# Row scales spread over the partitions by four small products with the identity, and row tiles loaded two to a buffer

## The chip, the cores and the metric

The kernel runs on one core of one Trainium2 chip. The metric is the device time of one execution in microseconds (us). Before the change three runs gave 842.63, 842.73 and 844.46 us; the median is 842.73 us.

## The reference, cut to what matters

One layer of an encoder trunk over 2048 rows (frames) of 1024 channels, all in float32:

```
h    = x * rsqrt(mean(x*x, axis=-1) + 1e-6) * norm_w        # RMSNorm, one scale per row
proj = h @ w_in                                             # 1024 -> 3348 columns, four branches
y_a, y_b, y_c, y_d = conv(...), gla(...), pool(...), ssd(...)
x    = x + concat(y_a, y_b, y_c, y_d) @ w_out
out  = x * rsqrt(mean(x*x, axis=-1) + 1e-6) * final_norm_w
```

The change touches only the first line: the scale `rsqrt(mean(x*x) + 1e-6)` of each row, and how it gets to where the projection's results are scaled. The branches (short causal convolutions, two chunked recurrences over chunks of 64 rows, moving means) matter only as the work that follows.

## The kernel before, in words

The 2048 rows are worked in two segments of 1024, each in two halves of 512 rows (f = 0 and 1). A float32 product is made as three products of "high" and "low" parts (`mm3`, L183): ACT casts an operand to its high part (L140) and DVE subtracts to get the low part (L141). A projection block (`block_ch`, L272) is 24 such products of 512 columns that put 128 channels by 512 rows into one of three accumulators (`acc`, L77). A block's result stays in its accumulator until DVE or ACT has moved it out (`evac`, L210).

The first segment doesn't wait for the row scales. Its operands are x * norm_w (`prep_first`, L521), and the scale is multiplied on behind the product: by row when rows lie on the partitions (`rt`, [row, tile], L621 and L624), and along the free axis, the same on all partitions, when channels lie on the partitions (`rb`, used in `evac` at L213 and L215). To get both, `scale_first` (L201) squares and sums four tiles of 128 rows on ACT (L199), takes 1/sqrt in a dozen small DVE steps (`rsqrt`, L121) and writes `rt` (L206). For `rb` it then sends the 512 numbers to a scratch tensor `rd` in DRAM by a DMA of POOL's queue (L207), and reads them back, the same 2 KB to each partition, by a DMA of SP's queue (L208), which waits until the first has landed.

The row tiles come in by `load_x` (L537). There are two buffers (tags "bt" and "cc", 8 KB a partition each), one tile of 4 KB a partition in each at a time, so that the third tile's load waits until the first tile's squares are done, and so on. The order in which the program emits the start is: x and weights of half 0 in pieces (L549 to L559), the q block's weights (L560), the first piece of half 1 (L561), two row tiles (L562), the parameters `prm` with the identity (L563), the products of the values and gates of half 0 (`kv_outer`, L566), two more row tiles (L581), `scale_first(0)`, the rest of half 1 (L584), and `scale_first(1)` with its four row tiles (L585). Then the segment loop runs: q block of half 0 and its `evac` with `rb` (L630), `kv_outer` of half 1, q block of half 1 and its `evac`, the B blocks, and so on.

For the second segment, whose operands are normalised before the product, `row_scale` (L228) sums the squares in the middle of the first segment and sends the scales to `rd` (L237), and `row_scale_bc` (L239) reads them back along the free axis (L241) when `prep` (L244) is about to use them (L595 and L746).

Each engine and each DMA queue works in order, and the order is fixed when the program is built: a planner takes the emitted instructions by their place in the program and by its own estimate of when each is ready, and so may put a later one ahead of an earlier one that isn't ready. `later` (L257) delays the emission of a piece by some projection blocks.

Of the kernel before, what the change touches and what calls it, by code (L numbers as in the profile page):

```python
# [35 lines left out]
           p_u=1808, p_z=2064, s_z=2320, xs=2576, B=2832, C=3088, dt=3344)  # L36
# channel-major blocks of 128 projection columns, in the order in which they are used
BLOCKS = ([('q', 0), ('B', 0), ('B', 1), ('k', 0), ('xs', 0), ('xs', 1), ('C', 0), ('C', 1)]
# [3 lines left out]

# columns of the packed per-channel parameters
PC = {}
# [9 lines left out]
def tile_hybrid_trunk(ctx: ExitStack, tc: tile.TileContext, xtok, xT, wkv, wch, wpu, wz, wo, pw_, nw, par, gw, fnw, out):  # L54
# [18 lines left out]
    def nm(s):  # L73
        uid[0] += 1
        return f"{s}_{uid[0]}"
# [9 lines left out]

# [1 line left out]
    # the tensor engine is kept at work until its first operands are there  # L87
    wz_ = px.tile([P, 512], F32, tag="xtok", name="warm")
# [27 lines left out]
    yd = dr.tile([SEQ // P, P, KD, P], F32, name="yd")  # L116
    rd = dr.tile([4, HALF], F32, name="rd")
    wd = dr.tile([2, P, D], F32, name="wd")

# [1 line left out]
    def rsqrt(ssq, inv, n, v=None):  # L121
        """1/sqrt(ssq*inv + EPS) of a [128, n] tile (or 1/sqrt(v)), times RS"""
        y = psm.tile([P, 16], F32, tag="ny", name=nm("ny"))[:, :n]
        a = psm.tile([P, 16], F32, tag="na", name=nm("na"), bufs=1)[:, :n]
        if v is None:
            v = psm.tile([P, 16], F32, tag="nv", name=nm("nv"), bufs=1)[:, :n]
            vec.tensor_scalar(v, ssq, inv, EPS, ALU.mult, ALU.add)  # L127
        vec.tensor_single_scalar(a.bitcast(I32), v.bitcast(I32), 1, ALU.logical_shift_right)
        vec.tensor_scalar(y.bitcast(I32), a.bitcast(I32), -1, 0x5f3759df, ALU.mult, ALU.add)
        for c in (3.0, 12.0, 768.0):  # L130
            if n == 1:
                vec.scalar_tensor_tensor(a, y, v, y, ALU.mult, ALU.mult)
            else:
                vec.tensor_tensor(a, y, v, ALU.mult)
                vec.tensor_tensor(a, a, y, ALU.mult)
            vec.scalar_tensor_tensor(y, a, c, y, ALU.subtract, ALU.mult)
        return y
# [5 lines left out]
    def load_w(src, n):  # L143
        """one packed weight tile [128, n] in its two parts"""
        raw = pw.tile([P, 1024], F32, tag="raw", name=nm("raw"), bufs=3)[:, :n]
        sp.dma_start(raw, src)
        return split_w(raw, n)
# [7 lines left out]
    def fold_pu(j):  # L155
        """p_u's projection block j with the pool's channel mixing folded into it, to wd"""
        raw = px.tile([P, KD, P], F32, tag="xT", name=nm("raw"))
# [25 lines left out]
    def mm3(o, ops):  # L183
        """o = sum of lhsT^T rhs over (lh, ll, rh, rl), each product in its three parts"""
        last = len(ops) - 1
# [15 lines left out]
    def scale_first(f, xs):  # L201
        """the 1/rms of four tiles of rows: [row, tile] to rt, and along the free axis on every partition to rb"""
        ssq = psm.tile([P, 4], F32, tag="ssq", name=nm("ssq"))
        square_sums(xs, ssq)
        rstd = rsqrt(ssq, 1.0 / D, 4)
        vec.tensor_single_scalar(rt[:, f, :], rstd, 1.0 / RS, ALU.mult)  # L206
        nc.gpsimd.dma_start(rd[f].rearrange("(j p) -> p j", p=P), rt[:, f, :])  # L207
        sp.dma_start(rb[:, f, :], rd[f:f + 1, :].to_broadcast([P, HALF]))  # L208

    def evac(s, f, dst, o, scale=None):  # L210
        """dst = o * scale of a channel-major block; the first segment's blocks still miss their rows' 1/rms"""
        if s == 0 and scale is None:
# [8 lines left out]
    def evac_silu(s, f, dst, o):  # L221
# [3 lines left out]
        else:  # L225
            act.activation(dst, o, AF.Silu)

    def row_scale(hf):  # L228
        """the rows' 1/rms of half hf (of four) to rd"""
        ssq = psm.tile([P, 4], F32, tag="ssq", name=nm("ssq"))  # L230
# [4 lines left out]
        rstd = rsqrt(ssq, 1.0 / D, 4)  # L235
        vec.tensor_single_scalar(rstd, rstd, 1.0 / RS, ALU.mult)
        nc.gpsimd.dma_start(rd[hf].rearrange("(j p) -> p j", p=P), rstd)  # L237

    def row_scale_bc(hf):  # L239
        rb = gen()[:, :512]  # L240
        sp.dma_start(rb, rd[hf:hf + 1, :].to_broadcast([P, HALF]))  # L241
        return rb

    def prep(s, f, rb):  # L244
        """normalised activations of half f of segment s, channel-major, in two parts"""
        hh, hl = hT[f] = big(f)
# [10 lines left out]
    def later(n, fn):  # L257
        """fn is emitted behind the n-th projection block from here"""
        queue.append([n, fn])
# [12 lines left out]
    def block_ch(f, w):  # L272
        """a projection block, channel-major: [128 channels, 512 tokens] of half f"""
        o = acc()
# [6 lines left out]
    def block_tok(tt, ws, n):  # L281
        """a projection block, token-major: [128 tokens, n columns]"""
        o = acc()[:, :n]
# [8 lines left out]
    def gate(f, kv):  # L292
        """decays [channel, token] of the keys of half f to the ends of their chunks, and the chunks' own decays"""
        lp = tr()
# [38 lines left out]
    def dt_chain(kv, wt, aD):  # L333
        """SSD step weights wt [tok, tt, head] and chunk decays aD [any, parity, tt, head]"""
        def t32(n):
# [31 lines left out]
    def ssd_conv(s, f, i, ps_):  # L367
        """silu(conv) of xbc block i for one half, channel-major"""
        xin = gen()
# [9 lines left out]
    def chunk_loop(kv, kt, q, aG, aD, bt, wxs, dxs, cc):  # L379
        """the updates of a token tile's two chunks, and a step later their outputs"""  # L380
        rows = (slice(0, CH), slice(CH, P))
# [51 lines left out]
    def spill(s, f, blk, y):  # L433
        """channel-major y [128, 512] of half f to block blk of the mixed channels"""
        t0 = s * TT + f * 4
# [34 lines left out]
    def pool_u(s, j, f, o):  # L470
        """mean over each window less the position's own value, of u already mixed"""
        lo_, hi_ = slice(0, 64), slice(64, 128)
# [42 lines left out]

# [1 line left out]
    # the first segment's products take x * norm_w and are scaled by the rows' 1/rms behind, which need not be waited for  # L517
    rb = pseg.tile([P, 2, HALF], F32, tag="rb", name="rb")
    rt = psm.tile([P, 2, 4], F32, tag="rt", name="rt", bufs=1)

    def prep_first(f, i, tag, n=2):  # L521
        """the first segment's activations of half f, channel tiles 2i and 2i+1, n at a time"""
        xt = px.tile([P, 2, HALF], F32, tag="xT", name=nm("xT"))
# [13 lines left out]
    def load_x(j, tag):  # L537
        xk = pseg.tile([P, D], F32, tag=tag, name=nm("xk"))
        sp.dma_start(xk, xtok[j])
        return xk  # L540

# [7 lines left out]
    for k0, k1 in order:  # L549
        next(x1[k0 // 2])  # L550
        k = k0
        while k < k1:
# [6 lines left out]
            k += n  # L559
    wq = load_w(wch[BLOCKS.index(('q', 0))], D)  # L560
    next(prep_first(1, 0, "wxs"))  # L561
    xh = [load_x(j, ("bt", "cc")[j % 2]) for j in range(2)]  # L562
    sp.dma_start(prm, par)  # L563
    act.activation(ea, pcol('alog', 0, 4), AF.Exp)

    def kv_outer(hs, o):  # L566
        """the values and gates of four token tiles, one k at a time"""
        for k in range(KD):
# [11 lines left out]
    kv_outer(hT[0], kvp)  # L580
    xh += [load_x(2 + j, ("bt", "cc")[j % 2]) for j in range(2)]  # L581
    scale_first(0, xh)
    for i in range(1, 4):
        next(prep_first(1, i, ("wxs", "dxs")[i % 2]))  # L584
    scale_first(1, [load_x(4 + j, ("bt", "cc")[j % 2]) for j in range(4)])  # L585

# [6 lines left out]
    for s in range(NSEG):  # L593
# [7 lines left out]
        wt = psm.tile([P, TT, 4], F32, tag="wt", name=nm("wt"), bufs=1)  # L601
        es, rsts = [], []
        cur = {} if s else {('q', 0): wq}
# [10 lines left out]
        for f in range(2):  # L614
# [14 lines left out]
            later(2, lambda f=f: rsts.append(gate(f, kv)))  # L629
            evac(s, f, q[:, f * HALF:(f + 1) * HALF], get('q', 0, f), 32.0 ** -0.5)  # L630
        later(2, lambda: gate_decay(rsts, aG, es))
# [75 lines left out]

        # gated outputs of the two recurrent branches
        wzt = []
# [30 lines left out]

        # pool, the first half of all its blocks before the second
        wp = []
        ab = {}
        for f in range(2):
# [4 lines left out]
            for j in range(2):  # L749
# [4 lines left out]
                if f == 1 and s + 1 < NSEG:  # L754
                    wk[0] = load_kv((0, 1)) if j == 0 else wk[0] + load_kv((2,))
# [1 line left out]
    fw = pseg.tile([P, D], F32, tag="kv", name="fw")  # L757
# [18 lines left out]
    def project(tt, c0, c1, i):  # L776
        """output columns c0:c1 of token tile tt with the residual, and their square sum; running mean square + EPS"""
        yh, yl, xk, r, ot, sq = tiles[tt]
# [35 lines left out]
def _pack(x, norm_w, w_in, conv_a_w, gla_gate_w, gla_gate_b, gla_norm_w, pool_w, pool_scale, ssd_conv_w, ssd_conv_b,  # L814
          ssd_dt_bias, ssd_a_log, ssd_d, ssd_norm_w, w_out, final_norm_w):
    """the inputs laid out for the kernel"""
    f = np.float32
# [72 lines left out]
```

## Time and profile before

| | |
|---|---|
| median of 3 runs | 842.73 us (842.63 to 844.46) |
| span of the profiled execution | 844.6 us |
| PE (matmul) busy | 816.5 us, 97% of the span |
| DVE busy | 499.3 us, 59% |
| ACT busy | 275.4 us, 33% |
| POOL busy | 6.3 us, 1% |
| mean granted clock of TensorE | 0.988 of full speed |
| DMA | 86.71 MB, mean 103 GB/s |

The profile is of one execution, whose own time is its span of 844.6 us; it is 1.9 us above the median of the runs. PE is the engine that sets the time. The slices of the profile cut the span in 40 pieces of 21.1 us; a digit is a busy share in tenths. A row of a timeline reads: start, duration, engine, source line, operation, output <- inputs, shape, count, and in brackets the idle time before it and what ended that. PE instructions overlap, so that the distance between starts, not the duration, says what one costs. A float32 product that isn't cut in parts shows as two records.

### The profile page before, as it was taken

To read this page: it belongs to the slowest core of one execution; us is meant where nothing else is said; L and a number is where in the kernel's file an instruction comes from. 1 tells how busy PE (TensorE), PEld (TensorE's weight loads), DVE (VectorE), ACT (ScalarE), POOL (GpSimd) and SP (SyncE) were. 2 spreads that over 40 slices of the span, in tenths; PEclk is the share of its full clock that TensorE was granted. 3 is DMA by queue.
4 is the path that set the end of the run, shared out by engine and by line. 5 is a ranking of instruction groups with operands and counts; after the bars stand their busy time and mean duration, and the time that the engine had idled before them with its cause. 6 is when DMAs were issued, how large, how long until landed. Compare 5 with 4: busy or idle time off the path is not lost.

```text
span 844.6 us, 11158 instructions
## 1 busy us (share of the span) xinstructions
PE 816.5 (97%) x4272; PEld 675.4 (80%) x4272; DVE 499.3 (59%) x1253; ACT 275.4 (33%) x487; POOL 6.3 (1%) x22
## 2 busy tenths in 40 slices
PE   7975999999999999999999999999999999999996
PEld 6954888787878888998888787878888888888885
DVE  5545757674754588955846464544578765555544
ACT  5633444242212332355545211213334332122211
POOL 0000000000000000000000000000000000000000
PEclk9987999999999999999999999999999999999999
DMA  8664101144741033523011102111045654443221
GB/s 283 231 158 115 47 29 51 51 148 119 117 135 38 26 116 113 190 61 125 26 51 50 50 27 75 45 44 38 25 162 165 181 191 151 150 150 124 101 100 50
DMA packets 38836, 86.71 MB, mean 103 GB/s; under 512 B 3872, under 2 KB 17536, under 8 KB 38784
## 3 DMA queue, kind: packets, MB, share of 16 engines
q1 hardware_dynamic: 38656, 86.00, 32.4%
q8 instruction: 33, 0.54, 0.3%
q14 instruction: 19, 0.16, 0.1%
q0 software_dynamic: 128, 0.01, 0.0%
HBM read 68.16 MB, written 17.83 MB: 102 GB/s over the span
## 4 chain that ended last, share of the span: by engine, by line
PE 86%; DMA 8%; DVE 2%; ACT 2%; issue 1%; SPq 1%; DVEq 0%; ACTq 0%
PE acc L187 27%; PE acc L189 27%; PE acc L188 27%; DMA xtok<-in_xtok 3%; DMA rd<-rt 2%; PE up L391 1%; PE tr L638 1%; PE oy L399 1%; PE oy L403 1%; DMA rb<-rd 1%; DMA xT<-in_xT 1%; DMA xk<-in_xtok 1%; ACT xtok L199 1%; DMA raw<-in_wkv 1%; PE tr L167 0%
## 5 line engine op out<-in xcount | busy, mean ns | idle before, releaser
L187 PE MATMUL acc<-bl,wh 128*128 128x512 f32 x640 | 255.6, 399 | 6.1 <-DVE nv L127 6.1
L189 PE MATMUL acc<-bh,wl 128*128 128x512 f32 x640 | 251.3, 393 | 0.0
L188 PE MATMUL acc<-bh,wh 128*128 128x512 f32 x640 | 251.1, 392 | 0.0
L187 PEld LDWEIGHTS acc<-bl,wh 128*128 128x128 f32 x640 | 121.3, 190 | 31.9 <-issue 6.3
L189 PEld LDWEIGHTS acc<-bh,wl 128*128 128x128 f32 x640 | 121.1, 189 | 26.0
L188 PEld LDWEIGHTS acc<-bh,wh 128*128 128x128 f32 x640 | 121.4, 190 | 23.9
L188 PE MATMUL acc<-bh,yh 128*128 128x512 f32 (+1 forms) x264 | 101.0, 383 | 0.0
L189 PE MATMUL acc<-bh,yl 128*128 128x512 f32 (+1 forms) x264 | 101.0, 383 | 0.0
L187 PE MATMUL acc<-bl,yh 128*128 128x512 f32 (+1 forms) x264 | 101.0, 383 | 0.0
L140 ACT CAST wh<-raw 128x1024 fp32r<-128x1024 f32 (+3 forms) x57 | 55.9, 982 | 119.6 <-PE acc L188 106.1
L141 DVE TENSOR_TENSOR wl<-raw,wh 128x1024 fp32r<-128x1024 f32 (+3 forms) x57 | 64.5, 1135 | 36.9 <-ACT wh L140 33.6
L187 PE MATMUL acc<-wl,bh 128*128 128x512 f32 (+1 forms) x192 | 69.0, 359 | 0.0
L189 PE MATMUL acc<-wh,bl 128*128 128x512 f32 (+1 forms) x192 | 68.5, 357 | 0.0
L188 PE MATMUL acc<-wh,bh 128*128 128x512 f32 (+1 forms) x192 | 68.4, 356 | 0.0
L376 DVE SCALAR_TENSOR_TENSOR g<-g,prm,g 128x512 f32<-128x512 f32 x72 | 53.7, 751 | 8.2 <-ACT g L374 6.7
L189 PEld LDWEIGHTS acc<-bh,yl 128*128 128x128 f32 x264 | 49.6, 188 | 9.7
L188 PEld LDWEIGHTS acc<-bh,yh 128*128 128x128 f32 x264 | 49.6, 188 | 9.7
L187 PEld LDWEIGHTS acc<-bl,yh 128*128 128x128 f32 x264 | 49.6, 188 | 9.7
L785 DVE TENSOR_TENSOR r<-acc,xk 128x512 f32<-128x512 f32 (+1 forms) x33 | 22.3, 675 | 56.2 <-PE acc L189 55.0
L786 ACT ACTIVATE xk<-r 128x512 f32<-128x512 f32 (+1 forms) x33 | 20.4, 618 | 86.8 <-issue 66.6
L187 PEld LDWEIGHTS acc<-wl,bh 128*128 128x128 f32 x192 | 36.1, 188 | 5.3 <-issue 0.3
L189 PEld LDWEIGHTS acc<-wh,bl 128*128 128x128 f32 x192 | 36.1, 188 | 5.2
(191 smaller groups left out, 872.8 us busy)
## 6 DMA issues: line engine op xcount, KB each, us to landing
raw<-in_wch SPq DMA_DIRECT2D x36, 512.0 KB, 3.4
xk<-in_xtok SPq DMA_DIRECT2D x24, 512.0 KB, 3.6
yr<-yd SPq DMA_DIRECT2D x16, 512.0 KB, 4.2
out<-ot SPq DMA_DIRECT2D x30, 256.0 KB, 2.2
xT<-in_xT SPq DMA_DIRECT2D x14, 512.0 KB, 4.4
xtok<-in_xtok SPq DMA_DIRECT2D x8, 512.0 KB, 6.4
raw<-in_wz SPq DMA_DIRECT2D x8, 512.0 KB, 3.9
yd<-g SPq DMA_DIRECT2D x16, 256.0 KB, 2.8
```

Source lines behind the costliest of these rows:

```text
L140: act.copy(hi, raw)
L141: vec.tensor_sub(lo, raw, hi.bitcast(F32))
L187: pe.matmul(o, lhsT=lh, rhs=rl, start=i == 0, stop=False)
L188: pe.matmul(o, lhsT=lh, rhs=rh, start=False, stop=False)
L189: pe.matmul(o, lhsT=ll, rhs=rh, start=False, stop=i == last)
L199: act.activation(xk, xk, AF.Square, accum_out=ssq[:, j:j + 1])
L376: vec.scalar_tensor_tensor(t, xin[:, k:k + 512], pcol('scw', 4 * i + k), t, ALU.mult, ALU.add)
L391: pe.matmul(o[:, CH + g * P:CH + (g + 1) * P], lhsT=bt[r, tt, g, :], rhs=wxs[r, tt, g * P:(g + 1) * P], start=True, stop=True)
L399: pe.matmul(oy[rows[i], 0:256], lhsT=q[:, tok[i]], rhs=st[i][0], start=True, stop=True)
L403: pe.matmul(oy[rows[i], 256 + g * P:256 + (g + 1) * P], lhsT=cc[:, g, tok[i]], rhs=st[i][1][:, gs], start=True, stop=True)
L785: vec.tensor_tensor(r[:, cs], o, xk[:, cs], ALU.add)
L786: act.activation(xk[:, cs], r[:, cs], AF.Square, accum_out=sq[:, i:i + 1])
```

## The change

The scales no longer go through DRAM. A new function makes four products: the left operand is one column of the scales [128 rows, 1], repeated 128 times along the free axis, and the right one is the identity; the result holds the 128 scales along the free axis on every partition. ACT copies the 512 results to SBUF. It is called four times: in the segment loop behind each q block of the first segment, and in `row_scale_bc` for each half of the second. A buffer of `load_x` now holds two row tiles, so that four row tiles fit at a time; their bytes and number of DMAs stay. The first four row tiles are loaded ahead of `kv_outer(hT[0], kvp)`, and `prm` ahead of the first piece of half 1.

```diff
...
-    rd = dr.tile([4, HALF], F32, name="rd")
...
         vec.tensor_single_scalar(rt[:, f, :], rstd, 1.0 / RS, ALU.mult)
-        nc.gpsimd.dma_start(rd[f].rearrange("(j p) -> p j", p=P), rt[:, f, :])
-        sp.dma_start(rb[:, f, :], rd[f:f + 1, :].to_broadcast([P, HALF]))
+
+    def along_rows(dst, cols):
+        tp = tr()
+        for j in range(4):
+            pe.matmul(tp[:, j * P:(j + 1) * P], lhsT=cols[:, j:j + 1].to_broadcast([P, P]), rhs=ident,
+                      start=True, stop=True)
+        act.copy(dst, tp)
...
+    scales = {}
+
     def row_scale(hf):
...
-        vec.tensor_single_scalar(rstd, rstd, 1.0 / RS, ALU.mult)
-        nc.gpsimd.dma_start(rd[hf].rearrange("(j p) -> p j", p=P), rstd)
+        scales[hf] = psm.tile([P, 4], F32, tag="rs", name=nm("rs"))
+        vec.tensor_single_scalar(scales[hf], rstd, 1.0 / RS, ALU.mult)
...
     def row_scale_bc(hf):
         rb = gen()[:, :512]
-        sp.dma_start(rb, rd[hf:hf + 1, :].to_broadcast([P, HALF]))
+        along_rows(rb, scales[hf])
         return rb
...
     def load_x(j, tag):
-        xk = pseg.tile([P, D], F32, tag=tag, name=nm("xk"))
-        sp.dma_start(xk, xtok[j])
-        return xk
+        xk = pseg.tile([P, 2, D], F32, tag=tag, name=nm("xk"))
+        for i in range(2):
+            sp.dma_start(xk[:, i, :], xtok[j + i])
+        return [xk[:, 0, :], xk[:, 1, :]]
...
     wq = load_w(wch[BLOCKS.index(('q', 0))], D)
+    sp.dma_start(prm, par)
     next(prep_first(1, 0, "wxs"))
-    xh = [load_x(j, ("bt", "cc")[j % 2]) for j in range(2)]
-    sp.dma_start(prm, par)
+    xh = load_x(0, "bt") + load_x(2, "cc")
...
     kv_outer(hT[0], kvp)
-    xh += [load_x(2 + j, ("bt", "cc")[j % 2]) for j in range(2)]
     scale_first(0, xh)
...
-    scale_first(1, [load_x(4 + j, ("bt", "cc")[j % 2]) for j in range(4)])
+    scale_first(1, load_x(4, "bt") + load_x(6, "cc"))
...
-            evac(s, f, q[:, f * HALF:(f + 1) * HALF], get('q', 0, f), 32.0 ** -0.5)
+            qs.append(get('q', 0, f))
+            if s == 0:
+                along_rows(rb[:, f, :], rt[:, f, :])
+            evac(s, f, q[:, f * HALF:(f + 1) * HALF], qs[f], 32.0 ** -0.5)
...
```

## Rows read from the trace of the kernel before

**Rows 1.** The page's slices of 21.1 us: PE's busy share, in tenths.
```profile
PE   7975999999999999999999999999999999999996
```

**Rows 2.** Timeline of PE, 27 to 85 us: blocks and waits.
```profile
27.63 0.29 PE L572 MATMUL acc<-wh,bh 128*128 128x276 f32 x1
...
39.76 0.40 PE L187 MATMUL acc<-bl,wh 128*128 128x512 f32 x1
...
45.26 0.60 PE L296 MATMUL tr<-prm,kv 128*16 128x128 f32 x4
51.91 0.76 PE L187 MATMUL acc<-bl,wh 128*128 128x512 f32 x1 [6.05 <-DVE nv L127]
...
56.31 0.42 PE L188 MATMUL acc<-bh,wh 128*128 128x512 f32 x1
...
74.84 0.79 PE L309 MATMUL tr<-rst,gst 96*128 96x512 f32 x1 [9.00 <-ACT rst L301]
...
80.12 0.46 PE L189 MATMUL acc<-bh,wl 128*128 128x512 f32 x1
```

**Rows 3.** Timeline of DVE, 25 to 72 us.
```profile
25.75 1.23 DVE L141 TENSOR_TENSOR bl<-xw,bh 128x1024 fp32r<-128x1024 f32 x1 [0.19 <-ACT bh L140]
...
35.12 0.17 DVE L206 TENSOR_SCALAR rt<-ny 128x4 f32<-128x4 f32 x1
...
51.07 0.69 DVE L215 SCALAR_TENSOR_TENSOR q<-acc,rb 128x512 f32<-128x512 f32 x1 [12.44 <-DMA rb<-rd]
...
71.30 0.69 DVE L215 SCALAR_TENSOR_TENSOR q<-acc,rb 128x512 f32<-128x512 f32 x1 [9.26 <-DMA rb<-rd]
```

**Rows 4.** The chain that ended last, 35 to 72 us: start, us, what.
```profile
35.59 10.72 DMA rd<-rt
...
55.59 9.84 DMA rd<-rt
65.45 5.83 DMA rb<-rd
```

**Rows 5.** Timeline of SP's queue, 12 to 47 us.
```profile
13.70 0.43 SPq L563 DMA_DIRECT2D prm<-in_par  x1
...
22.51 1.37 SPq L539 DMA_DIRECT2D xk<-in_xtok  x2
...
46.33 0.33 SPq L208 DMA_DIRECT2D rb<-rd  x1
```

**Rows 6.** Landing times of L539's DMAs, the row tiles, in us.
```profile
DMA to landing us min/median/max: 3.4/5.5/10.3
```

**Rows 7.** Stretches: engines busy (x count), PEclk, DMA share, GB/s.
```profile
16.00:20.00 4.00, 3.54 (x28) 3.54 (x29) 3.85 (x6) 2.03 (x3) 0.00 (x0) 1.00 1.00 390
...
40.00:44.00 4.00, 4.00 (x19) 3.29 (x18) 0.00 (x0) 0.00 (x0) 0.00 (x0) 1.00 0.00 0
...
52.00:56.00 4.00, 4.00 (x10) 3.13 (x11) 3.66 (x14) 2.78 (x4) 0.41 (x1) 0.50 0.73 298
```

**Rows 8.** Timeline of ACT, 21 to 48 us: squares of row tiles.
```profile
29.69 1.07 ACT L199 ACTIVATE xk<-xk 128x1024 f32<-128x1024 f32 x1
...
46.56 1.06 ACT L199 ACTIVATE xk<-xk 128x1024 f32<-128x1024 f32 x1 [7.83 <-DMA xk<-in_xtok]
```

**Rows 9.** Timeline of PE: four float32 products of 128 columns, and its neighbour.
```profile
208.12 1.16 PE L167 MATMUL tr<-g,raw 128*128 128x128 f32 x8
209.04 0.48 PE L187 MATMUL acc<-bl,wh 128*128 128x512 f32 x1
```

**Rows 10.** Chain in order of time: four transposes of 128 columns.
```profile
94.93 0.44 PE tr L638 x4
```

**Rows 11.** Line L363: loads of a left operand repeated along its free axis.
```profile
L363 PEld LDWEIGHTS tr<-d,prm x8: 185/189/192, 83.7 to 402.6; 128*128 128x128 f32 x8
```

**Rows 12.** Timeline of DVE, segment 1: the last operands of half 1.
```profile
367.59 1.36 DVE L141 TENSOR_TENSOR bl<-hf,bh 128x512 fp32r<-128x512 f32 x2
```

**Rows 13.** Timeline of PE, segment 1: last product of half 1's first block.
```profile
369.00 0.39 PE L189 MATMUL acc<-wh,bl 128*128 128x276 f32 x1
```

More of the change, by code (lines that the diff above doesn't have):

```diff
@@ L601, in tile_hybrid_trunk @@
         wt = psm.tile([P, TT, 4], F32, tag="wt", name=nm("wt"), bufs=1)
-        es, rsts = [], []
+        es, rsts, qs = [], [], []
         cur = {} if s else {('q', 0): wq}
```

## The prediction

> **What bounds the kernel now.** I read the page's slices first: PE is at nine tenths or more in 36 of 40 slices, and at seven, seven and five in the first, third and fourth [rows 1]. The change works in just that place, so everything else was read there. The timeline of PE then shows the two holes. After the q block of half 1, which ends at 45.26 us, come four short transposes, and then PE stands for 6.05 us before the first B block (51.91). After the second B block it stands for 9.00 us (74.84) [rows 2]. Together that is 15.05 us, more than half of the 28.1 us in which PE isn't busy (span less busy time).
>
> Why it stands is in DVE's timeline. The q blocks leave their accumulators by DVE's L215, which multiplies with `rb`. It waits 12.44 us for the read of `rd` at the first half and 9.26 us at the second [rows 3]. The accumulators are three, so the next block but one finds none free; and DVE works in order, so the steps of the gates behind L215 (L300, for which ACT and then L309 wait) are late too. The chain of waits gives the price of the trip: 10.72 and 9.84 us for POOL's write of 2 KB to DRAM, 5.83 us for the second read back [rows 4], which SP's queue issues only when the write has landed, at 46.33 for the first [rows 5]. Besides, after each hole TensorE is granted half its clock, 0.50 [rows 7]: 1.2 GHz in place of 2.4.
>
> **What goes.** The waits: 6.05 + 9.00 = 15.05 us. The slow stretches behind them: from 39.76 to 45.26 a block's 24 products take 5.50 us, 0.229 each, at the full clock; from 51.91 to 56.31 ten of the same products take 4.40 us where ten take 2.29, so 2.11 lost. From 74.84 to 80.12 it is one product of L309 (a first start interval of 0.59 us, so 0.30 at the full clock) and eleven more: 5.28 against 0.30 + 2.52 = 2.82, so 2.46 lost [rows 2]. In all 19.62 us, if nothing takes the holes' place. The four DMAs on POOL and the four reads on SP cost PE nothing else; SP's wait for the first write held up weights that PE did not lack.
>
> **What comes.** Four groups of four float32 products of 128 columns, all on PE, which has no idle time to hide them in once the holes are gone. The nearest rows are the four such products of L167: eight records, and the next block starts 0.92 us after the first of them [rows 9]. The left operand is a column repeated along its free axis; a load of this kind takes 189 ns at L363 [rows 11], as any other, so I take 0.92 a group, 3.68 us for four. Below, four transposes of 128 columns take 0.44 [rows 10], 1.76 in all; above, at half the clock, 1.84 a group, 7.36 in all. ACT's copy of 512 columns and L215 follow; they stand beside the next block's 5.5 us and, with three accumulators, cost nothing as long as they end inside it.
>
> **When the scales are there.** PE now has the products in its own in-order queue, so a late scale stops it directly; kv_outer, the next block and all behind them wait. Half 0's group is emitted behind the q block, which ends at 27.63 [rows 2]. In the trace the third and fourth row tiles were issued at 22.51, since their buffers held tiles whose squares were not done [rows 5]. Now they go out behind `prm`, about 14.1, 8.4 us earlier. They land 5.5 us (the median, [rows 6]) to, I estimate, 8 later, for the queues are full there (share 1.00 at 390 GB/s, [rows 7]): 20 to 22. Their squares are 1.07 us each on an ACT that has casts to do: done about 24 to 25. From the fourth tile's square, done about 30.8 [rows 8], to `rt` at 35.29 [rows 3] the small DVE steps took 4.5 us. So `rt` of half 0 is there at 28.5 to 29.5, 1 to 2 us after the q block. If the planner puts the group straight behind the block, PE waits that long; if it lets some of kv_outer go ahead, nothing. I take 1.0 us, with bounds of 0 and 2.5.
>
> For half 1 the four tiles need only the squares of the first four (done at 25), in place of each other's; with landing and 4.3 us of squares the last is done about 38, `rt` about 42. PE wants it when q's second block is done, 45.9 plus the 1.9 us that came before: 47.8. Covered by 5 us. In the trace the last square ran as late as 46.56, behind 7.83 us of waiting [rows 8]; but its load landed together with the `rd` write (46.33, [rows 5]), in a stretch in which no data moved at all (40 to 44: 0 GB/s, [rows 7]). With that write gone I expect a landing of 5.5 us.
>
> Moving 1 MB of row tiles ahead of half 1's remaining x costs those loads 2.7 us at 390 GB/s. The second piece's operands were ready at 26.98 [rows 3]; PE wants them two eighths into kv_outer, 27.63 + 2 x 1.52 = 30.7 [rows 2]. The 3.7 us of cover hold; if they didn't, a wait of up to 1 us would be seen, which the range takes in. Moving `prm`, a third of such a load, ahead of the first piece costs that piece less than the row tiles cost the next ones.
>
> In the second segment PE lacked nothing before, but half 1 is tight there: its last low part is made at 367.59 + 1.36 = 368.95 [rows 12] and PE uses it at 369.00 [rows 13]. DVE is still busy with the pool branch when PE and ACT make `rb`, so that doesn't delay it; and PE arrives 1.84 us later by its own two groups. Nothing, then, with up to 2 us either way should DVE's order change.
>
> A rule speaks against the change. The trace has 10.72 us for the 2 KB write and 5.83 for a read [rows 4]. The Trainium skill, "DMA: Bandwidth & Descriptors", section "Anatomy of one DMA — SWDGE (gpsimd) path", puts a DMA at about 2.0 us and a term of its bytes; by it the trip would take some 4.6 us (an estimate from that page), both scales would be there in time, and the change would only add its products. The trace doesn't agree: write and read alone are more than three times that, and DVE waited for them.
>
> **The sum.** 844.6 - 19.62 + 3.68 + 1.0 = 829.7 on the profiled execution, 14.9 less. That execution stood 1.9 above the median; the difference carried to the median gives 842.73 - 14.9 = 827.8.
>
> **The rivals.**
> A. The wait goes, but half 1's scales come late, and PE waits in its own queue. If the last square is done at 47.7 as in the trace, `rt` comes at 52.2: 4.4 us of waiting after 47.8, and 2.1 of slow clock after it: 827.8 + 6.5 = 834.3. For it: DVE's small steps wait in line, as in the trace. Against: nothing holds the load any more.
> B. The trip isn't the cause. Then the blocks waited for something that stays, such as weights queued on SP; nothing goes and 3.7 come: 846.4. For it: SP did stand behind L208. Against: L215 is the waiting instruction, twice, and `rb` what it waits for. (The price of the Trainium skill above would lead here.)
> C. Slower. Half 0's group stands straight behind the first q block, and its scales are late, since the planner puts the small DVE steps behind work that itself waits. Each us costs PE one; with 2.1 of slow clock the gain is used up when `rt` comes after 27.6 + 15.9 - 2.1 = 41.4. At 46, where the trace has the last square, it is 842.7 - 15.9 + 18.4 + 2.1 = 847.3. For it: in the trace half 0 had 18 us of cover, now none. Against: `rt` was there at 35.3 even with the late loads, and that would still be 4 us faster than before.
> D. Better: no wait at all, and products as short as the transposes: 842.73 - 19.62 + 1.76 = 824.9.
>
> **How the numbers follow.** The forecast (both holes gone, 825.5 to 830.5) 0.73, A 0.14, B 0.02, C 0.05, D 0.06. The time is 827.8. The range goes down past D's, to 824, and up to A's, to 834.5; outside remain B, C and a tail. A measurement here can tell 0.2%, 1.7 us, from no change: faster 0.93, same 0.02, slower 0.05.
>
> **What would show it.** Right: no `rd` rows; L215 waiting for PE or ACT for less than 2 us; PE without a hole over 2.5 us between 28 and 76, and its clock at 1.00 there; four groups of eight records of about 0.9 us; the first four row tiles issued by 15 us. Wrong: a wait of PE ahead of the new products (A or C, by the half), holes of the old size that end with a weight's cast (B), or a new wait near the second segment's start.

## The result, and the profile after

The changed kernel takes 829.94 us (median of 4 runs, 828.50 to 831.05), against 842.68 us (842.02 to 844.46) for the kernel before on the same chip: a ratio of 0.9843, 95% interval 0.9825 to 0.9860, or 12.7 us less. The forecast was 827.8 us, 14.9 less. Two more sets of runs on other chips give ratios of 0.9814 [0.9789, 0.9839] and 0.9793 [0.9779, 0.9806], which are 14.9 and 17.4 us. What differs among the chips is mostly the kernel before: its medians are 842.7, 845.4 and 846.5, the changed kernel's 829.9, 830.5 and 829.2.

The profiled execution of after has a span of 826.7 us, 17.9 less than that of before, and a time of 828.5. In this profiled execution and in those below the time stands 1.7 to 1.9 us above the span, so that the profiled execution of before was about 846.4 us in the metric (an estimate), some 3.7 above the median of its runs and above the slowest of them; it is nearer to the medians of the other chips. That of after was the fastest of its four, 1.4 below their median. That is why the profiles differ by more than the medians.

The page's slices of after: PE's busy share and the granted clock, in tenths.

```profile
PE   8999999999999999999999999999999999999996
PEclk9999999999999999999999999999999999999999
```

The seven, seven and five of [rows 1] are gone but for the first, now an eight. What PE waits for in the whole span of after, each row with total, times and longest in us:

```profile
PE acc L581 <- DVE bl L140: 1.6, 2, 1.0
PE warmp L92 <- DVE warm L89: 1.4, 1, 1.4
PE acc L581 <- ACT wh L139: 0.9, 1, 0.9
```

Neither hole of [rows 2] has a successor: these waits stand in the warm-up (L92) and in the first products of `kv_outer`, and the kernel before had them too. No row of after has `rd`, and no group of the new products waits. They are these four groups of eight records in the timeline of PE, each shown with the instruction that follows it, and ahead of them the first product of half 1's `kv_outer`:

```profile
27.53 0.29 PE L581 MATMUL acc<-wh,bh 128*128 128x276 f32 x1
...
31.38 1.16 PE L211 MATMUL tr<-prm,rt 128*128 128x128 f32 x8
32.30 0.37 PE L581 MATMUL up<-wh,bh 128*128 128x276 f32 x1
...
46.65 1.06 PE L211 MATMUL tr<-prm,rt 128*128 128x128 f32 x8
47.47 0.49 PE L186 MATMUL acc<-bl,wh 128*128 128x512 f32 x1
...
58.97 0.62 PE L316 MATMUL tr<-rst,gst 96*128 96x512 f32 x2
...
307.41 1.05 PE L211 MATMUL tr<-prm,rs 128*128 128x128 f32 x8
308.22 0.48 PE L186 MATMUL acc<-bl,wh 128*128 128x512 f32 x1
...
330.08 1.05 PE L211 MATMUL tr<-prm,rs 128*128 128x128 f32 x8
330.88 0.37 PE L186 MATMUL acc<-wl,bh 128*128 128x276 f32 x1
```

From start to start a group costs 0.92, 0.82, 0.81 and 0.80 us, 3.35 together. The first stands inside `kv_outer`, among its products (L581 on both sides of it): the planner let 3.85 us of `kv_outer` (27.53 to 31.38) go ahead of it, and so PE did not stand for it. The row at 58.97 is the pair of products between which PE stood for 9.00 us before. The timeline of DVE in after shows when the small steps of half 0 begin (L126), when the scales are there (L205) and when the q blocks leave (L220, with no wait in brackets):

```profile
26.69 0.17 DVE L126 TENSOR_SCALAR nv<-ssq 128x4 f32<-128x4 f32 x1 [4.08 <-ACT xk L198]
...
31.16 0.17 DVE L205 TENSOR_SCALAR rt<-ny 128x4 f32<-128x4 f32 x1
...
34.66 0.68 DVE L220 SCALAR_TENSOR_TENSOR q<-acc,rb 128x512 f32<-128x512 f32 x1
...
40.72 0.17 DVE L205 TENSOR_SCALAR rt<-ny 128x4 f32<-128x4 f32 x1
...
50.20 0.69 DVE L220 SCALAR_TENSOR_TENSOR q<-acc,rb 128x512 f32<-128x512 f32 x1
```

The multiplication that waited until 51.07 and 71.30 [rows 3] starts at 34.66 and 50.20. From SP's queue of after, the row of the first four row tiles:

```profile
12.81 2.13 SPq L548 DMA_DIRECT2D xk<-in_xtok  x4
```

And the stretches of after from 40 to 44, in which the kernel before moved nothing, and from 42.5 to 51, where it had its first hole; columns as in [rows 7]:

```profile
40.00:44.00 4.00, 4.00 (x22) 3.40 (x22) 2.90 (x10) 3.02 (x7) 0.00 (x0) 1.00 0.49 134
42.50:51.00 8.50, 8.50 (x45) 7.03 (x44) 7.60 (x20) 4.84 (x8) 0.00 (x0) 1.00 0.82 266
```

PE is busy all through and its clock is at 1.00, that is 2.4 GHz; 134 and 266 GB/s move.

### The profile page after: what moved, and what is told of

Read it like the earlier page. It is cut to its first block, busy times and chain, and to the rows that moved or that the text cites. A ratio compares the mean times of both kernels' runs of the same rounds, so it can differ in the third digit from the quotient of the medians.

```text
span 826.7 us, 11204 instructions
## 1 busy us (share of the span) xinstructions
PE 815.3 (99%) x4304; PEld 676.9 (82%) x4304; DVE 499.2 (60%) x1253; ACT 277.2 (34%) x491; POOL 3.1 (0%) x18
## 4 chain that ended last, share of the span: by engine, by line
PE 97%; DMA 1%; DVE 1%; SPq 0%; ACT 0%; issue 0%; DVEq 0%; ACTq 0%
PE acc L186 30%; PE acc L188 29%; PE acc L187 29%; PE up L398 1%; PE oy L406 1%; PE up L581 1%; PE tr L649 1%; PE oy L410 1%; PE acc L581 1%; DMA xT<-in_xT 1%; DMA raw<-in_wkv 1%; PE oy L581 1%; PE up L394 1%; PE tr L166 0%; PE tr L211 0%; PE tr L708 0%
```

## Experiments

They ran on several chips, each set beside the kernel before on the same chip. A ratio is to that.

**One part alone.** Two kernels split the change: the products with the old loads, and the loads with the old trip. The first:

```diff
-        xk = pseg.tile([P, 2, D], F32, tag=tag, name=nm("xk"))
-        for i in range(2):
-            sp.dma_start(xk[:, i, :], xtok[j + i])
-        return [xk[:, 0, :], xk[:, 1, :]]
+        xk = pseg.tile([P, D], F32, tag=tag, name=nm("xk"))
+        sp.dma_start(xk, xtok[j])
+        return xk
...
+    next(prep_first(1, 0, "wxs"))
+    xh = [load_x(j, ("bt", "cc")[j % 2]) for j in range(2)]
     sp.dma_start(prm, par)
-    next(prep_first(1, 0, "wxs"))
-    xh = load_x(0, "bt") + load_x(2, "cc")
...
+    xh += [load_x(2 + j, ("bt", "cc")[j % 2]) for j in range(2)]
...
```

> The scales by products, but the row tiles one to a buffer and in the old order. Theory (the trip through DRAM held PE, the loads matter little): rt of half 0 comes at about 35.3 us, as before, rt of half 1 at about 45 to 46, since no rd write delays the last row tile; PE waits 0 to 1.5 us ahead of each group. Time 829 to 833 us, at most 3 us above the changed kernel. Rival (the earlier loads do much of it): a wait of 4 us or more ahead of the second group, with half the clock behind it; 836 us or more.

It took 829.04 us against 846.67: 0.9793 [0.9778, 0.9807]. It ran a second time on a chip with the changed kernel beside it:

> The products with the old loads, once more, now beside the changed kernel on one chip. In its first runs it took 829.0 us, where the changed kernel took 829.9 and 830.5 in others. Theory (the loads are worth nothing once the trip is gone): within 1 us of the changed kernel. Rival (the early loads save the 1.1 us that PE waited for the first group): 1 us or more slower than it.

> The changed kernel on the same chip as the three others of this group: 829 to 831 us, as in its earlier runs.

That gave 829.50 us, 0.9796 [0.9783, 0.9810], and 829.15 us, 0.9793 [0.9779, 0.9806] for the changed kernel: with the products in place the early loads are worth nothing that these runs can tell. In both profiles of the first kernel half 0's scales come only at about 35, and half 1's at about 45, and the planner puts each group about where they are there: in the first profile PE stands 1.11 us for half 0's, in the second it doesn't. The loads without the products:

```diff
-        xk = pseg.tile([P, D], F32, tag=tag, name=nm("xk"))
-        sp.dma_start(xk, xtok[j])
-        return xk
+        xk = pseg.tile([P, 2, D], F32, tag=tag, name=nm("xk"))
+        for i in range(2):
+            sp.dma_start(xk[:, i, :], xtok[j + i])
+        return [xk[:, 0, :], xk[:, 1, :]]
...
```

> The row tiles two to a buffer and early, the trip through DRAM kept. Theory: rt of half 0 comes at 31 us in place of 35.3, so the first hole shrinks from 6 to about 2 us, and the second stays near 9, since the trip of half 1 starts only when rt of half 1 is made behind L215. Gain 4 to 6 us: 837 to 839. Rival (the loads do most): both holes gone, 830 or less. Rival (loads do nothing): 842 to 843.

It took 845.32 us, 0.9989 [0.9976, 1.0002]. I had expected half 0's scales, 4 us earlier, to be worth as much; they were not. (The loads are called where the change calls them.) The timeline of DVE in this kernel, the two evacuations of the q blocks:

```profile
47.23 0.69 DVE L215 SCALAR_TENSOR_TENSOR q<-acc,rb 128x512 f32<-128x512 f32 x1 [8.67 <-DMA rb<-rd]
...
66.75 0.69 DVE L215 SCALAR_TENSOR_TENSOR q<-acc,rb 128x512 f32<-128x512 f32 x1 [9.49 <-DMA rb<-rd]
```

They are 3.8 and 4.6 us earlier than in [rows 3]. But PE stands in more places, as its timeline shows:

```profile
35.79 0.39 PE L573 MATMUL acc<-wh,bl 128*128 128x276 f32 x1 [1.58 <-DVE bl L141]
...
49.94 0.50 PE L187 MATMUL acc<-bl,wh 128*128 128x512 f32 x1 [2.25 <-DVE ny L136]
...
51.91 0.79 PE L189 MATMUL acc<-bh,wl 128*128 128x512 f32 x1 [1.23 <-DVE wl L141]
...
67.43 0.50 PE L309 MATMUL tr<-rst,gst 96*128 96x512 f32 x1 [2.83 <-ACT rst L301]
...
72.97 0.80 PE L309 MATMUL tr<-rst,gst 96*128 96x512 f32 x1 [5.04 <-ACT rst L301]
```

Two of these five, 1.58 and 1.23, are waits for operands, not for `rb`. The timeline of ACT shows that two more hang on weights, and the stretch from 36 to 40 what moved while the write was under way:

```profile
48.84 1.04 ACT L140 CAST wh<-raw 128x1024 fp32r<-128x1024 f32 x1 [9.54 <-DMA raw<-in_wch]
...
65.74 1.04 ACT L140 CAST wh<-raw 128x1024 fp32r<-128x1024 f32 x1 [10.87 <-DMA raw<-in_wch]
```

```profile
36.00:40.00 4.00, 4.00 (x33) 4.00 (x33) 1.44 (x3) 3.14 (x5) 0.00 (x0) 1.00 0.00 0
```

The product at 49.94 needs the high part that ACT had ready at 49.88 (its releaser in brackets is a DVE step that ended at the same moment), and the L301 for which PE waited 2.83 us stood on ACT behind the second of these casts, whose weights were issued at 51.88, 0.9 us behind the second write, and took 13.8 us to land. Only the last wait, 5.04, stands behind `rb` (L215 at 66.75). SP's queue issued the read of `rd` at 42.55, when the write from 31.62 had landed, nothing from 29.9 until then, and the B blocks' weights behind it (43.88). That is why nothing moved from 36 to 40: nothing had been asked for. So an earlier trip only moved the 0 GB/s ahead, and the weights became late.

**Is it POOL's queue?** The writes of `rd` issued by SP in place of POOL (`sp.dma_start` for `nc.gpsimd.dma_start`, at both places):

> The kernel before with the write to rd issued on SP's queue in place of POOL's; all else as before. If the 10 us of the write are the price of POOL's queue: the write lands in 2 to 4 us, rb of half 0 is there before 45 us, the first hole goes and the second shrinks to about 2: 826 to 832 us, without any product. If they are the price of 512 scattered writes of 4 bytes on any queue: holes as before, 841 to 845 us.

859.98 us, 1.0159 [1.0139, 1.0178], 13.3 us slower than before and outside both of my ranges. The chain of waits in this kernel has the same price of the write:

```profile
36.17 11.79 DMA rd<-rt
...
56.43 10.82 DMA rd<-rt
```

And the extra time has a place, at one of the two writes for segment 1; first SP's queue in this kernel, then PE's timeline:

```profile
209.77 0.38 SPq L237 DMA_DIRECT2D rd<-ny  x1
210.20 0.50 SPq L161 DMA_DIRECT2D g<-in_pw_  x1
```

```profile
220.48 2.05 PE L167 MATMUL tr<-g,raw 128*128 128x128 f32 x8 [10.91 <-DMA g<-in_pw_]
```

A 64 KB load issued 0.43 us behind the write released PE only at 220.48, ten us later, where the write too would land by its 10.8 to 11.8; PE stood 10.91 us for it, and from 215 to 225 its clock was at 0.50, which is 1.2 GHz. PE's rows in the two kernels stand level at L357 (83.15 and 83.12) and 15.1 us apart at the second group of L167 (214.58 and 229.72). So the write is as slow from either queue, and a load issued behind it lands late. The page's count of packets on SP's queue rises by 40,768 - 38,656 = 2,112, which is 528 for each of the four writes, 16 more than its 512 numbers: they go one by one. On POOL's queue the page counts 128 packets for the four writes of the kernel before, 32 each, so that there the count doesn't show it.

The kernel before, where POOL writes, has such late loads too. The chain of waits has a row tile of 512 KB that was issued 2.7 us behind the write of 186.69. Below it stand DVE's first step that waits for its squares, and PE's wait for a later step of DVE:

```profile
189.39 11.75 DMA xtok<-in_xtok
```

```profile
202.41 0.17 DVE L127 TENSOR_SCALAR nv<-ssq 128x4 f32<-128x4 f32 x1 [9.45 <-ACT xtok L199]
```

```profile
206.19 0.43 PE L399 MATMUL oy<-sb,q 128*64 128x256 f32 x1 [0.34 <-DVE sb L412]
```

The row tiles loaded in this stretch (140 to 215) land within 5.6 us in after, which has no such write, and within 5.3 in the kernel of the next experiment, which writes in larger pieces. And in the kernel before a 64 KB load issued at 211.20, 2.5 us behind the write of 208.66, took 12.0 us to land, where one of the same line issued at 204.25 took 2.7.

**The pieces.** The kernel before, with `rd` laid out so that each partition's four scales stand side by side: 128 pieces of 16 bytes in place of 512 of 4, at both writes (one is shown). It leaves out the putting in order: the read stays, and so the scales reach the wrong rows.

```diff
-        nc.gpsimd.dma_start(rd[f].rearrange("(j p) -> p j", p=P), rt[:, f, :])
+        nc.gpsimd.dma_start(rd[f].rearrange("(p j) -> p j", p=P), rt[:, f, :])
```

> The kernel before with the write to rd in another order: each partition's four scales go to four neighbouring numbers (16 bytes in one piece, 128 pieces), not to four places 512 bytes apart (512 pieces of 4 bytes). The read stays, so the scales reach the wrong rows; nothing else changes. If the 10 us are the price of the many small pieces: the write lands in 3 to 5 us, the first hole goes, the second shrinks to 3 or less: 826 to 832. If they are the price of any such write: as before, 843 to 847.

830.77 us, 0.9815 [0.9799, 0.9831], beside 829.15 for the changed kernel on the same chip. This is nearly all that the change gains, with the trip through DRAM, the old loads and no product. Its chain of waits has both writes of the first segment:

```profile
35.52 3.42 DMA rd<-rt
...
48.23 4.09 DMA rd<-rt
```

The same bytes take 3.42 and 4.09 us where [rows 4] have 10.72 and 9.84. POOL's queue counts 128 packets as before, so the pieces show in the landing alone; whether it is their number or their size that counts, this experiment doesn't tell. SP's queue issues the read at 38.96 and the weights behind it from 39.34, and from 40 to 44 this kernel moves 183 GB/s:

```profile
40.00:44.00 4.00, 4.00 (x19) 3.29 (x19) 0.27 (x1) 1.15 (x2) 0.00 (x0) 1.00 0.92 183
```

The first hole is gone, the second is halved; PE's timeline of this kernel has only this between 40 and 80:

```profile
62.02 0.79 PE L309 MATMUL tr<-rst,gst 96*128 96x512 f32 x1 [4.36 <-ACT rst L301]
```

The last experiment puts the scales in order again, and has the early loads: the read goes to a temporary tile, and ACT copies it with a stride.

```diff
+    def from_rd(dst, hf):
+        t = gen()[:, :512]
+        sp.dma_start(t, rd[hf:hf + 1, :].to_broadcast([P, HALF]))
+        act.copy(dst.rearrange("q (j p) -> q j p", j=4), t.rearrange("q (p j) -> q j p", j=4))
```

> The kernel before with the changed kernel's loads (four row tiles early), the trip through DRAM kept for all four halves, but written in 128 pieces of 16 bytes instead of 512 of 4, and put in order behind the read by ACT's copy of 512 elements with a stride. No products on PE, and right scales. My theory: the holes came from the write in 4-byte pieces, which took 10 to 12 us and in which no other load landed, and not from the trip as such. Half 0's scales stand at 31.2 us; with a write of 3.5, a read of 6 and a copy of 0.8 us rb is there at about 42, ahead of the end of q's second block at 46. Half 1's scales come at about 45, rb at 56, 6 us ahead of the block that wants the accumulator. Then both holes are gone and PE has no group to do (3.35 us less than the changed kernel): 825.5 to 828 us, ratio to before about 0.976 to 0.979. Rival one: SP's queue stands at rb's read ahead of the B weights, as with the loads alone, and a wait for a weight's cast of 1 to 5 us stays at 36 to 50 us: 829 to 832. Rival two: the reads wait for other loads and hole two stays at 4 us as with the 16-byte pieces and old loads: 830 to 831. Rival three: a trip through DRAM loses whatever its pieces: 843 to 846.

829.74 us against 844.65, 0.9829 [0.9808, 0.9850]. My 825.5 to 828 was too low, though the main point held. Its chain of waits:

```profile
30.90 5.13 DMA rd<-rt
36.05 4.70 DMA g<-rd
40.77 1.10 ACT rb L204
...
45.60 3.42 DMA rd<-rt
49.04 4.85 DMA g<-rd
53.91 1.11 ACT rb L204
```

`rb` is there at 41.9 and 55.0, as expected (42 and 56). But the second hole closed only in part: PE's timeline has

```profile
60.26 0.79 PE L314 MATMUL tr<-rst,gst 96*128 96x512 f32 x1 [3.35 <-ACT rst L306]
```

and from 60 to 64 a clock of 0.57. Rival two named this wait, with its cause wrong: the reads were not late. Behind the scales at 55.0 DVE still had the q block, small steps of the SSD branch (`dt_chain`), the next block's evacuation and the `rst` step in line, the last of them done at 59.6. The products bring half 1's q block out at 50.20, 4.9 us earlier than this trip does. No median tells this kernel from the changed one: their intervals overlap.

**What a group costs.** The four products of each group made three times over (`for j in (0, 1, 2, 3) * 3`), eight groups more:

> Each of the four groups makes its four products three times over into the same place; the results are the same. Theory: eight more groups of 0.85 to 0.92 us each on PE, 6.8 to 7.4 us more than the changed kernel: 836 to 838. Rival (PE has slack behind the holes that takes them up): less than 4 us more.

835.90 us, 0.9877 [0.9853, 0.9901], just under my 836 to 838, beside the changed kernel on the same chip:

> The changed kernel once more, beside the two below: 828 to 831 us, as in its first runs.

830.45 us, 0.9814 [0.9789, 0.9839]. Eight groups more cost 5.45 us by the medians, 0.68 each. PE's timeline of the tripled kernel has for half 1's group

```profile
47.93 2.84 PE L211 MATMUL tr<-prm,rt 128*128 128x128 f32 x24
50.53 0.49 PE L186 MATMUL acc<-bl,wh 128*128 128x512 f32 x1
```

2.60 us from start to start, 1.78 more than the 0.82 of a single group: 0.89 for each four products, 7.1 for eight. The 1.7 us between the two are not given back behind the groups: PE's rows of the two profiles drift apart by 1.8 us at each of the four (from 1.45 us ahead in front of the first to 5.69 behind after the last) and by nothing elsewhere. The tripled kernel was 1.45 us ahead in the first products of `kv_outer`, where the profiles of one and the same kernel differ too (by up to 0.9 us among the three of the changed one). So the trace's price holds, 3.35 us for the four groups of the change; the medians alone would say 2.7.

**The place of the first group.** `kv_outer` of half 1 held behind the first group, as rival C had it:

```diff
-                    kv_outer(hT[1], kvp)
+                    with tc.issue_after(grp.ins):
+                        kv_outer(hT[1], kvp)
...
-                along_rows(rb[:, f, :], rt[:, f, :])
+                grp = along_rows(rb[:, f, :], rt[:, f, :])
```

> The changed kernel with half 1's kv_outer held behind the first group of products, so that the group stands right behind the first q block at 27.5 us. rt of half 0 comes at 31.3 us. Theory (a late scale now stops PE directly, in its own queue): PE stands 3.7 us there, where the changed kernel does not stand; 3.5 to 4.5 us above the changed kernel, 2 us more if the clock falls behind the wait. Rival (the planner's place is worth nothing, PE would have waited later anyway): the same time as the changed kernel, within 1 us.

834.23 us, 0.9852 [0.9837, 0.9867], against 829.04 for the products with old loads on the same chip and 829.2 to 830.5 for the changed kernel on others: some 4 to 5 us lost. PE's timeline and the stretches of this kernel:

```profile
30.96 2.08 PE L211 MATMUL tr<-prm,rt 128*128 128x128 f32 x8 [3.89 <-DVE rt L205]
32.69 0.58 PE L582 MATMUL acc<-wh,bh 128*128 128x276 f32 x1
```

```profile
28.00:32.00 4.00, 1.04 (x5) 1.04 (x6) 3.86 (x14) 2.88 (x4) 0.00 (x0) 0.80 0.73 232
32.00:36.00 4.00, 4.00 (x27) 4.00 (x27) 3.04 (x7) 2.92 (x5) 0.00 (x0) 0.78 1.03 406
```

PE waits 3.89 us for `rt`, and the group behind the wait takes 1.73 us in place of 0.92, its clock granted at half for part of that. C's mechanism is real; the planner avoided it.

**Segment 1's scales by DRAM again.** The change with the old trip for `row_scale` and `row_scale_bc` alone (L237 and L241 of before put back), with the early loads and, in a second kernel, with the old ones:

> The changed kernel, but the second segment's scales go through DRAM again as in the kernel before, where nobody waited for them. Theory (each group costs PE its 0.9 us and hides behind nothing): 1.8 us less than the changed kernel, 826.5 to 829. Rival (the groups hide, or the slow write disturbs the loads beside it): the same within 0.5 us, or slower.

> Old loads, products for the first segment alone, the second segment's scales through DRAM. Theory (two groups of 0.8 to 0.9 us less on PE, loads worth nothing): 1.7 us less than the products with the old loads, 827 to 829. Rival (the slow write of the second segment holds up loads that PE needs): the same or slower.

828.16 us, 0.9792 [0.9766, 0.9817], beside 830.45 for the changed kernel; and 829.36 us, 0.9799 [0.9786, 0.9812], beside 829.50 for the products with old loads. The first says 2.3 us gained, the second 0.1, where I had expected 1.8 and 1.7. The traces show two sides. The two groups left out give 1.7 us back in each. But the write of segment 1 again makes loads late (a row tile took 11.5 and 12.9 us to land), and PE falls back behind them by 0.8 us in the first kernel and by 1.5 in the second, both between 175 and 191. The trip itself has time in segment 1; the loads behind its write have not. Some 0.9 and 0.2 us are left; what more there is in the 2.3 stays open.

## Why the prediction was right, point by point

**The mechanism** was the predicted one: `rb` came late, DVE's L215 stood for it, the accumulators stayed full and DVE's gate steps came late; with the scales there in time both holes went, and the half clock with them. The shift between the two profiles grows as the terms say: at L357 of before (83.15, now 64.91) it is 18.24, against 15.05 + 4.57 of holes and slow clock less two groups of 0.92 and 0.82, 17.88. At the first products of L167 it is 19.1 (208.12 and 189.0), and the two groups of segment 1 bring it down to 17.5 (389.76 and 372.27 at the gates' transposes). The one us more has no term in my sum. It is gained between 205.21 and 207.47 of before, at PE's wait of 206.19, shown above: a row tile behind the first write of segment 1 was late, and DVE's steps for PE late with it. In the kernel with 16-byte pieces the shift against before rises at the same place, from 13.9 to 14.9. So the prediction's sentence that the DMAs on POOL and SP cost PE nothing else was wrong by 1.0 us.

**The sum's terms.** Removed, 19.62: right in the trace of before, but for the 1.0 us of segment 1, which makes it 20.6. Added, 3.68: measured 3.35. The wait of 1.0 us at the first group: measured 0, for the planner put it inside `kv_outer`, the second of the two possibilities that I had named. With the measured terms the sum gives 844.6 - 20.6 + 3.35 = 827.4 us for the span; 826.7 was measured, where I had forecast 829.7. So the profiles gained 17.9 us in place of 14.9, and the medians 12.7. The sum was carried from one execution to the median as if the holes were the same in each; the profiled execution was 3.7 us above the median, not 1.9, since its time was taken as its span, and that of after 1.4 below. That the excess lay in the holes is an inference: no profile of a faster execution of before was taken. The two errors, 3.0 us too little gained in the span and 5.2 too much carried to the median, lie on opposite sides: that 827.8 came within 2.1 us of the measured median is in part luck.

Half 0's `rt` was forecast for 28.5 to 29.5 and was there at 31.33, though the tiles were issued at 12.81. DVE's small steps took 4.6 us, as forecast (4.5); it was ACT's squares that were done at 26.6 and not at 24 to 25, with copies and a cast in line between them. With the group where I had it in the sum, that would have cost 3.89, as the experiment on its place shows, and not 1.0 or at most 2.5. Half 1's `rt` was forecast for 42 and was there at 40.89; needed at 46.65.

**The part of the loads** was taken for needed, so that half 0's scales would be in time. It was not: with the old loads the scales come some 4 us later and the planner again puts the group about where they are there, at a wait of 1.1 us in one profile and none in the other, and at no cost that the medians tell (829.50 and 829.15 on one chip). The loads' own costs (x late, `prm` ahead) were nothing, as forecast.

**The price of the trip.** The prediction said that "SP's wait for the first write held up weights that PE did not lack". In before that is so: the first B block's weights had been issued at 31.26, ahead of the read, and of those behind it the first were ready at 55.20, for a block that began at 75.43. With the loads early the read stood ahead of the first B block's weights on SP's queue (42.55 and 43.88), and the same wait cost PE 2.25 us for their high part and 1.23 for the low. And 10.72 us were read as the price of a trip through DRAM. They are the price of 512 pieces of 4 bytes: in pieces of 16 the same 2 KB landed in 3.4 to 5.1 us over the four writes of the first segment, and in 1.7 to 4.4 over those of the second. The Trainium skill, "DMA: Bandwidth & Descriptors", section "Anatomy of one DMA — SWDGE (gpsimd) path", has about 2.0 us and the bytes, for a DMA of POOL's path; the prediction took it for SP's read as well. The 16-byte writes took 0.9 to 2.6 times that, the 4-byte ones about five to six times; the measurement decides. The same page's section "Rules for kernel authors" says that a strided last dimension becomes one descriptor for each element. The 528 packets of each write on SP's queue agree with that, and the rows give its price here: 6 to 7 us a write, and the loads behind it.

**The rivals.** A (half 1's scales late): not so, 5.8 us of cover (40.89 to 46.65). B (the trip isn't the cause): wrong as put, since the holes went with the trip and no weight kept them open; yet a trip in larger pieces would have done as well. C: its place and its price were confirmed by force, and not met; by its own terms an `rt` at 35.3 would have been 6.1 us faster than before (41.4 less 35.3), not 4. D's lower end, 824.9: not reached. Its products are 1.6 us too cheap (1.76 for 3.35), which in the profiles the 1.0 us of segment 1 and some scatter make up; the 5 us to 829.9 lie in carrying the gain of one execution to the median.

## What to carry to other kernels

When a chain of waits shows a small DMA at several times the landing of large ones, look at its access pattern before replacing it: here a layout of the scratch that lets a partition write its four numbers together gave what the products on PE gave. A long small DMA costs twice, by its own landing and by the loads that are issued behind it and land late. And a product whose operand comes late is free only where the order of PE's queue lets other work go ahead of it.

## What had not been expected of the hardware

A 2 KB write in 4-byte pieces takes 9.6 to 11.8 us from POOL's queue or SP's, and loads issued behind it on SP's queue land late: a row tile at the start of before after 10.3 us, the longest of [rows 6], though 0 GB/s moved in the second half of that; row tiles of segment 1 after 11.5 to 12.9 and a 64 KB load after 12.0. With 16-byte pieces, or no such write, the row tiles of segment 1 land within 5.6. The stretches without data, 0 GB/s from 40 to 44 in before and from 36 to 40 in the kernel with early loads, are another matter: SP's queue stood at the read and asked for nothing. A wait of PE of 3.89 us in the start was followed by a granted clock of 0.78 over the next stretch (32 to 36), and one of 3.35 ahead of 60.26 by 0.57 (60 to 64): for a part of each PE ran at 1.2 GHz in place of 2.4, and the short holes were dear too.
